# Feed-forward products in another order, and 32-byte pads in four pools

## The chip, the cores and the metric

One Trainium2 chip, one core of it. The metric is the time of one execution on the device in microseconds (us). A core has five engines with queues of their own: PE (TensorE, matrix products; PEld is its loading of weights, which overlaps), DVE (VectorE), ACT (ScalarE), POOL (GpSimd) and SP (SyncE, which here issues most transfers). Each engine takes its instructions strictly in its own order, and waits where an operand isn't there.

## The reference

Two blocks over 512 positions of width 1024, in float32. The first block projects the normed input (`p = h @ w_in`), runs a causal convolution of width 31 with a layer norm, an RWKV scan over 16 heads, and three output products. The second block has two layers, each of attention and of a feed-forward part:

```python
def conv_ffn(h, w_up, conv_w, conv_b, w_down):
    Tp = h.shape[1]
    u = h @ w_up
    up = jnp.pad(u, ((0, 0), (CONV_W - 1, 0), (0, 0)))
    c = conv_b + sum(up[:, j:j + Tp] * conv_w[j] for j in range(CONV_W))
    gate, val = jnp.split(c, 2, axis=-1)
    return (jax.nn.silu(gate) * val) @ w_down
```

`w_up` is 1024 x 5632 and `w_down` 2816 x 1024; the convolution has width 3 and runs along the positions.

## The kernel before, in words

Activations lie transposed: 128 channels on the partitions, positions along the row (512 in the first block, 528 with the 16 meta tokens in the second; the last layer computes 512 of them). Each float32 operand is split in two fp32r parts, hi and lo, and a product is three matmuls: lo weights with hi data, hi weights with lo data, hi with hi (`mm3`, L247; the line of the call that issues a matmul is L75). Weights come in tiles of at most 128 x 1024 (`weights`, L204): SP loads `wst`, ACT casts it to `wh` (L212), POOL subtracts to get `wl` (L215). There are 2, 3 and 3 buffers of these, so a tile's cast waits until the tile three before it has been used up.

The first block (`block1`) multiplies with 512 columns at a time. Its moving operands are the tiles `hx` (the normed input, for the 73 output tiles of `w_in`, the first seven of which are named `pg` in the trace), `ch`, `yo` and `mx` (the operands of `w_conv_out`, `w_rwkv_out` and `w_out`). While these run, the convolution is made on DVE (`cy<-u,vec,cy`, 30 instructions for each of 8 tiles) and the RWKV scan on all engines, in small steps that wait for each other.

`ffn` (L1565) runs once per layer. Its 44 tiles of `w_up` are taken in pairs j = 0 to 21: a gate tile into the PSUM banks `g` and a value tile into the banks `pt`, two banks each. DVE scales them out of PSUM into `u` (L163), ACT and DVE make the convolution `c` (L176, then L173 twice), ACT the tanh `t`, DVE and POOL the product (`t<-t,c` on POOL, L163), ACT casts it to the hi part of `f` (L1604) and DVE subtracts to get the lo part (L163). `f` has 26 buffers, 13 pairs. The inner dimension is done in two parts of 11 pairs: 11 times up, then 8 output tiles m of `w_down`, then again 11 times up and 8 output tiles. One output tile is 11 steps of the inner dimension, in two weight tiles of 6 and 5 steps (128x768 and 128x640), with three matmuls per step: 66 matmuls of 264 columns in layer 0, 33 of 512 columns in layer 1. The tiles m alternate between the banks `g` and `pt`; `add_h` adds a finished one to the residual on DVE. The order of PE in the second block is that of the program; the other engines' order comes from a scheduler.

SBUF is shared out by pools that lie one behind the other, and a tile takes a multiple of 32 bytes per partition. In the built program `hx`, `ch`, `yo` and `mx` of the first block start 32 bytes past a multiple of 64, and all tiles `f` at a multiple of 64.

Of the kernel before, what the change touches and what calls it, by code (L numbers as in the profile page):

```python
# [7 lines left out]
F32 = mybir.dt.float32  # L8
F32R = mybir.dt.float32r
AF = mybir.ActivationFunctionType  # L10
OP = mybir.AluOpType
# [3 lines left out]
P = 128  # L15
S = 512
NT = 8
# [10 lines left out]
NF = 2 * D_FF // P  # L28
# [104 lines left out]
class Kern:  # L133
    def __init__(self, ctx, tc, A, dump):
        self.ctx, self.tc, self.nc, self.A, self.dump = ctx, tc, tc.nc, A, dump
        self.pe = Weave(tc.nc)
        nc = self.nc
        self.cp = ctx.enter_context(tc.tile_pool(name="cp", bufs=1))
        self.vec = self.cp.tile([P, NVEC], F32, name="vec")
        self.con = self.cp.tile([P, NCON], F32, name="con")  # L140
        self.mhalf = self.cp.tile([P, 1], F32, name="mhalf")
        nc.vector.memset(self.mhalf, -0.5)

    def load(self):
        self.nc.sync.dma_start(self.con, self.A["con"])
# [191 lines left out]
def block1(K):  # L337
    nc, tc, A = K.nc, K.tc, K.A
# [31 lines left out]
    hx = []  # L370
    with tc.tile_pool(name="ps0", bufs=1, space=PSUM) as ps0:
# [3 lines left out]
        with tc.high_priority(offset=150000):  # L375
# [3 lines left out]
            for q in range(2):  # L379
                p = pg[5 + q]  # L380
                nc.tensor.matmul(p, one[0:1], row[:, q * 512:(q + 1) * 512], start=True, stop=True)
                th = K.slot("e")
# [19 lines left out]
        for k in range(NT):  # L402
            with tc.high_priority(offset=120000 if k < 2 else 0):
# [3 lines left out]
                gs, sh, x = gsc[:, k:k + 1], mod[:, k:k + 1], xs[k]  # L407
                stt(gs, mod[:, 8 + k:9 + k], 1.0, K.v("norm_g", k), OP.add, OP.mult)
                if k < 2:
                    stt(x, x, gs, rstd, OP.mult, OP.mult)  # L410
                    hi, lo = K.slot("hx", F32R), K.slot("hx", F32R)
# [9 lines left out]
                wh, wl = K.weights(A["w_in0"][k], lo="p")  # L421
# [75 lines left out]

    K.pe.finish(norm)
    ch = [conv.out_gate(i, cog[i]) for i in range(NT)]
    m_ = []  # L500
    for i in range(NT):
        th = K.slot("sq")
# [12 lines left out]
    for i in range(NT):  # L515
        th = K.slot("th")
# [140 lines left out]
class Rwkv:  # L657
# [41 lines left out]
    def close(self):  # L699
        self.rctx.close()  # L700
# [245 lines left out]
    def done(self, what, i):  # L946
        s = self.streams.get((what, i))
        return i < 0 or s is not None and s.done
# [83 lines left out]
class Block2:  # L1032
# [193 lines left out]
    def tl(self, tag, bufs, shape=(P, T), dt=F32):  # L1226
        return self.ap.tile(list(shape), dt, name=tag, tag=tag, bufs=bufs)
# [337 lines left out]
    def ffn(self, l, hx, acc, done):  # L1565

        K, nc, A = self.K, self.nc, self.A
        o = N_META if l else 0
        n, o2 = T - o, max(o - 2, 0)
        mid = (o + T) // 2  # L1570
        hin = [slice(o2, mid), slice(mid, T)]
        hout = [slice(0, n)] if n <= 512 else [slice(0, n // 2), slice(n // 2, n)]
        rb = K.slot("rb")
        p0 = self.first(self.rstd(acc, rb), (A["w_up"][l, 0], hx), (A["w_up"][l, 1], hx), halves=hin)
        with self.tc.tile_pool(name=f"ff{l}", bufs=1, reuse_waits="tile") as fp:
            def tl(tag, bufs, w=n, dt=F32):
                return fp.tile([P, w], dt, name=tag, tag=tag, bufs=bufs)

            half = NF // 4
            banks = self.g, self.pt  # L1580
            for part in range(2):
                fx = []
                for j in range(part * half, (part + 1) * half):
                    c = []
                    for q in range(2):
                        p = p0[q] if j == 0 else self.gemm(A["w_up"][l, 2 * j + q], hx, bank=banks[q], halves=hin)
                        u = tl("u", 3, n + 2)
                        if o == 0:
                            nc.gpsimd.memset(u[:, 0:2], 0.0)
                        for ph, sl in zip(p, hin):  # L1590
                            K.tt(u[:, sl.start + 2 - o:sl.stop + 2 - o], ph, rb[:, sl], OP.mult)
                        f = j + q * (NF // 2)
                        cw = [K.v("conv_w_2", (l * 3 + t) * NF + f) for t in range(3)]
                        x = tl("c", 4)
                        K.act(x, u[:, 2:], AF.Identity, bias=K.v("conv_b_2", l * NF + f), scale=cw[2])
                        K.stt(x, u[:, 0:n], cw[0], x, OP.mult, OP.add)
                        K.stt(x, u[:, 1:n + 1], cw[1], x, OP.mult, OP.add)
                        c.append(x)
                    th = tl("t", 2)
                    K.act(th, c[0], AF.Tanh, scale=0.5)  # L1600
                    K.stt(th, th, 1.0, c[0], OP.add, OP.mult)
                    K.tt(th, th, c[1], OP.mult, "p")
                    hi, lo = tl("f", 26, dt=F32R), tl("f", 26, dt=F32R)
                    nc.scalar.copy(hi, th)  # L1604
                    K.tt(lo, th, hi, OP.subtract)
                    fx.append((hi, lo))
                k0, kn = part * half, 6
                for m in range(NT):
                    ps = [banks[m % 2]()[:, :n // len(hout)] for _ in hout]
                    for a, b in ((0, kn), (kn, half)):  # L1610
                        wh, wl = K.weights(A["w_down"][l, m][:, (k0 + a) * P:(k0 + b) * P], lo="p")
                        for q in zip(ps, hout):
                            K.gemm([q], wh, wl, fx[a:b], first=a == 0, last=b == half)
                    self.add_h(m, ps, 0.5, o)
                    if part == 1:
                        done(m)


    def layer_b(self, hq, acc):
# [249 lines left out]
def body(tc, A, out, dump=None, stop=None):  # L1869
    with ExitStack() as ctx:  # L1870
        K = Kern(ctx, tc, A, dump)
        K.wb = (2, 3, 3)
        K.wp = ctx.enter_context(tc.tile_pool(name="wp", bufs=3))
        K.rw = ctx.enter_context(tc.tile_pool(name="rw", bufs=1))
        K.rd = ctx.enter_context(tc.tile_pool(name="rd", bufs=1, space=DRAM))
        if stop == 2:
            hp = K.hp = ctx.enter_context(tc.tile_pool(name="hp", bufs=1, side="right"))
            K.h = [hp.tile([P, T], F32, name=f"h{i}") for i in range(NT)]
            K.hxt = (ctx.enter_context(tc.tile_pool(name="hxp", bufs=1, side="right", reuse_waits="tile")), T, 16)
            K.load()  # L1880
            K.b1 = ExitStack()
            p0 = K.b1.enter_context(tc.tile_pool(name="b0", bufs=1))
            with tc.tile_pool(name="b1", bufs=1, space=PSUM) as p1:
                bank = lambda: p1.tile([P, 512], F32, name="p", tag="p", bufs=2)
                bias_rows(K, p0.tile([P, 1024], F32, name="st"), bank)
                meta(K, bank)
            K.tags = {"acc": (p0, S, 2), "sq": (p0, S, 2)}
            st = dict(acc=("acc", "acc"), sq="sq", x=[])
            for i in range(NT):
                tc.nc.sync.dma_start(K.h[i][:, N_META:], A["x1"][i])  # L1890
                start(K, st, i)
        else:
            st = block1(K)
        if stop == 1:
            K.b1.close()
            return
        block2(K, out, ctx, st)
# [111 lines left out]
```

## Time and profile before

| | us |
|---|---|
| median of 3 runs | 2368.82 (2368.64 to 2380.41) |
| the profiled execution | 2374.06 |
| its span, first to last instruction | 2372.1 |
| PE busy | 2166.3 (91%) |
| DVE, POOL, ACT busy | 1503.0, 1180.5, 875.4 |

The span is one execution's trace, on which everything below rests; about 2 us lie around it. "Busy" of PE is a sum over pipelined matmuls, so it hides short gaps. The first block takes about the first 916 us, layer 0's feed-forward part runs from about 1186 to 1590 us and layer 1's from about 1970 to the end.

### The profile page before, as it was taken

What the parts mean: (1) busy time and instruction counts of PE and PEld (TensorE: products, weight loads), DVE (VectorE), ACT (ScalarE), POOL (GpSimd) and SP (SyncE); (2) the same over time, 40 slices, a digit from 0 to 9 for tenths busy, and PEclk for the clock granted to TensorE, in tenths of its full rate; (3) what the DMA queues carried; (4) which work ended last, traced back from release to release, by engine and by line L of the source; (5) the groups of instructions that cost most, each with busy time, mean ns of one, the idle gap of its engine ahead of it and who ended that gap; (6) DMA issues with size and microseconds to landing.
All of it is one profiled execution on the core that took longest, in us unless ns stands there. A gap on an engine that the chain in (4) does not pass through costs nothing. (4 is left out here: it accounts for less than half of the span.)

```text
span 2372.1 us, 38579 instructions
## 1 busy us (share of the span) xinstructions
PE 2166.3 (91%) x15069; PEld 1883.9 (79%) x15069; DVE 1503.0 (63%) x2675; ACT 875.4 (37%) x1739; POOL 1180.5 (50%) x989
## 2 busy tenths in 40 slices
PE   5998989997999998998999899898668899989989
PEld 4766766764677777997999899897568799979987
DVE  8477986899972476998466346531366766642661
ACT  3333232332243333535333223332255663332331
POOL 5485556566634446344545445463433345444443
PEclk9998999998999999999999999999789999999999
DMA  7522222222343654220222232232211012223223
GB/s 252 163 71 61 63 83 61 64 68 56 87 154 126 240 167 135 73 63 10 65 82 84 79 97 85 71 102 73 60 58 43 31 63 90 82 78 108 81 76 102
DMA packets 114540, 213.86 MB, mean 90 GB/s; under 512 B 47229, under 2 KB 50813, under 8 KB 114358
## 3 DMA queue, kind: packets, MB, share of 16 engines
q1 hardware_dynamic: 111380, 208.29, 28.1%
q10 hardware_dynamic: 2978, 3.10, 0.4%
q8 instruction: 119, 1.95, 0.3%
q14 instruction: 63, 0.52, 0.1%
HBM read 193.32 MB, written 20.64 MB: 90 GB/s over the span
## 5 line engine op out<-in xcount | busy, mean ns | idle before, releaser
L215 POOL TENSOR_TENSOR wl<-wst,wh 128x1024 fp32r<-128x1024 f32 (+4 forms) x315 | 704.7, 2238 | 725.6 <-ACT wh L212 595.7
L75 PE MATMUL g<-hx,wh 128*128 128x264 f32 (+3 forms) x3680 | 883.3, 329 | 6.6 <-DVE hx L173 6.6
L75 PEld LDWEIGHTS g<-hx,wh 128*128 128x128 f32 x3680 | 622.8, 195 | 62.8 <-issue 11.7
L75 PE MATMUL g<-hx,wl 128*128 128x264 f32 (+3 forms) x1840 | 600.0, 329 | 35.1 <-DVE u L173 9.5
L212 ACT CAST wh<-wst 128x1024 fp32r<-128x1024 f32 (+4 forms) x315 | 304.4, 966 | 421.3 <-PE g L75 223.7
L75 PEld LDWEIGHTS g<-hx,wl 128*128 128x128 f32 x1840 | 356.3, 195 | 61.4 <-issue 11.1
L173 DVE SCALAR_TENSOR_TENSOR c<-u,vec,c 128x528 f32<-128x528 f32 (+1 forms) x176 | 244.7, 1391 | 83.3 <-ACT c L176 81.6
L75 PE MATMUL pt<-hx,wh 128*128 128x264 f32 (+2 forms) x1504 | 271.6, 283 | 0.0
L173 DVE SCALAR_TENSOR_TENSOR cy<-u,vec,cy 128x512 f32<-128x512 f32 x240 | 239.0, 1004 | 3.8
L75 PEld LDWEIGHTS pt<-hx,wh 128*128 128x128 f32 x1504 | 230.2, 189 | 0.0
L75 PE MATMUL pt<-hx,wl 128*128 128x264 f32 (+2 forms) x752 | 207.5, 285 | 10.9 <-DVE u L163 10.8
L75 PEld LDWEIGHTS pt<-hx,wl 128*128 128x128 f32 x752 | 139.2, 189 | 13.2 <-POOL wl L215 10.0
L75 PE MATMUL g<-f,wh 128*128 128x264 f32 (+1 forms) x528 | 123.5, 329 | 2.9 <-DVE f L163 2.9
L75 PE MATMUL pt<-f,wh 128*128 128x264 f32 (+1 forms) x528 | 121.3, 324 | 0.0
L75 PE MATMUL g<-f,wl 128*128 128x264 f32 (+1 forms) x264 | 87.0, 330 | 20.3 <-ACT f L1604 20.3
L75 PEld LDWEIGHTS g<-f,wh 128*128 128x128 f32 x528 | 90.5, 195 | 11.1 <-DVE f L163 4.5
L75 PEld LDWEIGHTS pt<-f,wh 128*128 128x128 f32 x528 | 89.6, 192 | 7.4
L1604 ACT CAST f<-t 128x528 fp32r<-128x528 f32 (+1 forms) x44 | 27.6, 627 | 181.1 <-POOL t L163 96.2
L163 POOL TENSOR_TENSOR t<-t,c 128x528 f32<-128x528 f32 (+1 forms) x44 | 57.5, 1307 | 67.0 <-DVE c L173 67.0
L75 PE MATMUL pt<-f,wl 128*128 128x264 f32 (+1 forms) x264 | 85.8, 325 | 0.0
L176 ACT ACTIVATE t<-c 128x528 f32<-128x528 f32 (+1 forms) x44 | 28.1, 638 | 139.9 <-DVE c L173 139.9
L163 DVE TENSOR_TENSOR f<-t,f 128x528 fp32r<-128x528 f32 (+1 forms) x44 | 35.3, 802 | 68.7 <-ACT f L1604 68.7
(411 smaller groups left out, 3849.8 us busy)
## 6 DMA issues: line engine op xcount, KB each, us to landing
wst<-in_w_up SPq DMA_DIRECT2D x88, 512.0 KB
wst<-in_w_in SPq DMA_DIRECT2D x66, 512.0 KB
ast<-in_ada_w SPq DMA_DIRECT2D x24, 512.0 KB
wst<-in_w_down SPq DMA_DIRECT2D x32, 384.0 KB
wst<-in_w_down SPq DMA_DIRECT2D x32, 320.0 KB
wst<-in_w_in_a SPq DMA_DIRECT2D x17, 512.0 KB
wst<-in_w_kv_b SPq DMA_DIRECT2D x16, 512.0 KB
hrb<-rw_d SPq DMA_DIRECT2D x18, 264.0 KB
```

The lines of the kernel that those rows point to most:

```text
L75: self.nc.tensor.matmul(out, lhsT, rhs, **kw)
L163: (self.nc.vector if eng == "v" else self.nc.gpsimd).tensor_tensor(out, a, b, op)
L173: self.nc.vector.scalar_tensor_tensor(out, a, s, b, op0=o1, op1=o2, accum_out=accum)
L176: self.nc.scalar.activation(out, a, f, bias=bias, scale=scale, accum_out=accum)
L212: nc.scalar.copy(wh[:, :n], st[:, :n])
L215: (nc.vector if lo == "v" else nc.gpsimd).tensor_tensor(wl[:, :n], st[:, :n], wh[:, :n], OP.subtract)
L1604: nc.scalar.copy(hi, th)
```

## The change

`up(j)`, `open_down`, `weights`, `down` and `close` are the old loop's parts as functions. Then:

1. Twelve pairs go up ahead of the first part's output tiles, not eleven; the twelfth (j = 11) belongs to the second part. After these tiles come the ten pairs that are left.
2. In the second part the output tiles m = 0 and 1 both take steps 0 to 9 of the inner dimension, and then the last step each; their four weight tiles are asked for in one go.
3. `line` takes 32 bytes of a pool, and POOL sets them to zero: in `rw` (after which everything in the left half of SBUF lies 32 bytes further), in `cv` (where `ch` lies) and in `ff0` and `ff1` (the pools of `ffn`, where `f` lies). Four such instructions are added.

In the built program the moving operands `hx`, `ch`, `yo` and `mx` of the first block now start at a multiple of 64 bytes, all 2328 matmuls that read them; `f` starts there as before, and the operands of 264, 258 and 256 columns stand where they stood with respect to 64. No other instruction changes its place on its engine, apart from single swaps of neighbours.

```diff
--- before.py
+++ after.py
@@ -140,6 +140,10 @@
         self.con = self.cp.tile([P, NCON], F32, name="con")
         self.mhalf = self.cp.tile([P, 1], F32, name="mhalf")
         nc.vector.memset(self.mhalf, -0.5)
+
+    def line(self, pool):
+
+        self.nc.gpsimd.memset(pool.tile([P, 8], F32, name="line"), 0.0)
 
     def load(self):
         self.nc.sync.dma_start(self.con, self.A["con"])
@@ -497,6 +501,7 @@
 
     K.pe.finish(norm)
     ch = [conv.out_gate(i, cog[i]) for i in range(NT)]
+    K.line(cv)
     m_ = []
     for i in range(NT):
         th = K.slot("sq")
@@ -1576,44 +1581,80 @@
             def tl(tag, bufs, w=n, dt=F32):
                 return fp.tile([P, w], dt, name=tag, tag=tag, bufs=bufs)
 
+            K.line(fp)
             half = NF // 4
             banks = self.g, self.pt
+
+            def up(j):
+
+                c = []
+                for q in range(2):
+                    p = p0[q] if j == 0 else self.gemm(A["w_up"][l, 2 * j + q], hx, bank=banks[q], halves=hin)
+                    u = tl("u", 3, n + 2)
+                    if o == 0:
+                        nc.gpsimd.memset(u[:, 0:2], 0.0)
+                    for ph, sl in zip(p, hin):
+                        K.tt(u[:, sl.start + 2 - o:sl.stop + 2 - o], ph, rb[:, sl], OP.mult)
+                    f = j + q * (NF // 2)
+                    cw = [K.v("conv_w_2", (l * 3 + t) * NF + f) for t in range(3)]
+                    x = tl("c", 4)
+                    K.act(x, u[:, 2:], AF.Identity, bias=K.v("conv_b_2", l * NF + f), scale=cw[2])
+                    K.stt(x, u[:, 0:n], cw[0], x, OP.mult, OP.add)
+                    K.stt(x, u[:, 1:n + 1], cw[1], x, OP.mult, OP.add)
+                    c.append(x)
+                th = tl("t", 2)
+                K.act(th, c[0], AF.Tanh, scale=0.5)
+                K.stt(th, th, 1.0, c[0], OP.add, OP.mult)
+                K.tt(th, th, c[1], OP.mult, "p")
+                hi, lo = tl("f", 26, dt=F32R), tl("f", 26, dt=F32R)
+                nc.scalar.copy(hi, th)
+                K.tt(lo, th, hi, OP.subtract)
+                return hi, lo
+
+            def open_down(m):
+                return [banks[m % 2]()[:, :n // len(hout)] for _ in hout]
+
+            def weights(part, m, a, b):
+                k0 = part * half
+                return K.weights(A["w_down"][l, m][:, (k0 + a) * P:(k0 + b) * P], lo="p")
+
+            def down(ps, w, fx, a, b, c, first=False, last=False):
+
+                for q in zip(ps, hout):
+                    K.gemm([q], *w, fx[a:b], first=first, last=last, k0=a - c)
+
+            def close(part, m, ps):
+                self.add_h(m, ps, 0.5, o)
+                if part == 1:
+                    done(m)
+
+            kn = 6
+            fx = [up(j) for j in range(half + 1)]
             for part in range(2):
-                fx = []
-                for j in range(part * half, (part + 1) * half):
-                    c = []
-                    for q in range(2):
-                        p = p0[q] if j == 0 else self.gemm(A["w_up"][l, 2 * j + q], hx, bank=banks[q], halves=hin)
-                        u = tl("u", 3, n + 2)
-                        if o == 0:
-                            nc.gpsimd.memset(u[:, 0:2], 0.0)
-                        for ph, sl in zip(p, hin):
-                            K.tt(u[:, sl.start + 2 - o:sl.stop + 2 - o], ph, rb[:, sl], OP.mult)
-                        f = j + q * (NF // 2)
-                        cw = [K.v("conv_w_2", (l * 3 + t) * NF + f) for t in range(3)]
-                        x = tl("c", 4)
-                        K.act(x, u[:, 2:], AF.Identity, bias=K.v("conv_b_2", l * NF + f), scale=cw[2])
-                        K.stt(x, u[:, 0:n], cw[0], x, OP.mult, OP.add)
-                        K.stt(x, u[:, 1:n + 1], cw[1], x, OP.mult, OP.add)
-                        c.append(x)
-                    th = tl("t", 2)
-                    K.act(th, c[0], AF.Tanh, scale=0.5)
-                    K.stt(th, th, 1.0, c[0], OP.add, OP.mult)
-                    K.tt(th, th, c[1], OP.mult, "p")
-                    hi, lo = tl("f", 26, dt=F32R), tl("f", 26, dt=F32R)
-                    nc.scalar.copy(hi, th)
-                    K.tt(lo, th, hi, OP.subtract)
-                    fx.append((hi, lo))
-                k0, kn = part * half, 6
-                for m in range(NT):
-                    ps = [banks[m % 2]()[:, :n // len(hout)] for _ in hout]
-                    for a, b in ((0, kn), (kn, half)):
-                        wh, wl = K.weights(A["w_down"][l, m][:, (k0 + a) * P:(k0 + b) * P], lo="p")
-                        for q in zip(ps, hout):
-                            K.gemm([q], wh, wl, fx[a:b], first=a == 0, last=b == half)
-                    self.add_h(m, ps, 0.5, o)
-                    if part == 1:
-                        done(m)
+                f, m0 = fx[:half], 0
+                if part == 0:
+
+                    fx = fx[half:]
+                else:
+
+                    two = []
+                    for m in range(2):
+                        ps, w = open_down(m), weights(1, m, 0, kn)
+                        down(ps, w, f, 0, kn, 0, first=True)
+                        w = weights(1, m, kn, half)
+                        down(ps, w, f, kn, half - 1, kn)
+                        two.append((ps, w))
+                    for m, (ps, w) in enumerate(two):
+                        down(ps, w, f, half - 1, half, kn, last=True)
+                        close(1, m, ps)
+                    m0 = 2
+                for m in range(m0, NT):
+                    ps = open_down(m)
+                    down(ps, weights(part, m, 0, kn), f, 0, kn, 0, first=True)
+                    down(ps, weights(part, m, kn, half), f, kn, half, kn, last=True)
+                    close(part, m, ps)
+                if part == 0:
+                    fx += [up(j) for j in range(half + 1, 2 * half)]
 
 
     def layer_b(self, hq, acc):
@@ -1872,6 +1913,7 @@
         K.wb = (2, 3, 3)
         K.wp = ctx.enter_context(tc.tile_pool(name="wp", bufs=3))
         K.rw = ctx.enter_context(tc.tile_pool(name="rw", bufs=1))
+        K.line(K.rw)
         K.rd = ctx.enter_context(tc.tile_pool(name="rd", bufs=1, space=DRAM))
         if stop == 2:
             hp = K.hp = ctx.enter_context(tc.tile_pool(name="hp", bufs=1, side="right"))
```

Where layer 1's first part ends, on PE. The names: `hx` is the normed input, `f_19836` and `f_19837` are hi and lo of pair 0. Before:

```order
L75 MATMUL pt_21140<-hx_19677,wl_21111 128x256
L75 MATMUL pt_21140<-hx_19678,wh_21110 128x256
L75 MATMUL pt_21140<-hx_19677,wh_21110 128x256
L75 MATMUL g_21180<-f_19836,wl_21183 128x512
L75 MATMUL g_21180<-f_19837,wh_21182 128x512
L75 MATMUL g_21180<-f_19836,wh_21182 128x512
```

And now, behind the same product (pair 10's second tile):

```order
L75 MATMUL pt_21148<-hx_19683,wl_21119 128x256
L75 MATMUL pt_21148<-hx_19684,wh_21118 128x256
L75 MATMUL pt_21148<-hx_19683,wh_21118 128x256
L75 MATMUL g_21194<-hx_19396,wl_21190 128x258
L75 MATMUL g_21194<-hx_19397,wh_21189 128x258
L75 MATMUL g_21194<-hx_19396,wh_21189 128x258
```

The 96 matmuls of pair 11 have moved in between pair 10 and the first output tile.

Where the first output tile of layer 1's second part ends, on PE. `f_23026` is the hi part of pair 21 before, `f_23034` now; `g_` and `pt_` are the output tiles m = 0 and 1. Before:

```order
L75 MATMUL g_23030<-f_22892,wh_23056 128x512
L75 MATMUL g_23030<-f_23026,wl_23057 128x512
L75 MATMUL g_23030<-f_23027,wh_23056 128x512
L75 MATMUL g_23030<-f_23026,wh_23056 128x512
L75 MATMUL pt_23078<-f_21686,wl_23081 128x512
```

And now the end of tile 1's steps 0 to 9 and what follows:

```order
L75 MATMUL pt_23081<-f_22900,wh_23107 128x512
L75 MATMUL g_23038<-f_23034,wl_23065 128x512
L75 MATMUL g_23038<-f_23035,wh_23064 128x512
L75 MATMUL g_23038<-f_23034,wh_23064 128x512
L75 MATMUL pt_23081<-f_23034,wl_23108 128x512
L75 MATMUL pt_23081<-f_23035,wh_23107 128x512
L75 MATMUL pt_23081<-f_23034,wh_23107 128x512
L75 MATMUL g_23134<-f_21318,wl_23137 128x512
```

The first matmul that reads pair 21 stood 30 matmuls behind the last up product, and stands 60 behind it now.

The same place on POOL, from the last weight tile of `w_up` on. Before (`t_22888` and `t_23022` belong to pairs 20 and 21):

```order
L215 TENSOR_TENSOR wl_22961<-wst_22959,wh_22960 128x1024
L215 TENSOR_TENSOR wl_23033<-wst_23031,wh_23032 128x768
L163 TENSOR_TENSOR t_22888<-t_22888,c_22884 128x512
L215 TENSOR_TENSOR wl_23057<-wst_23055,wh_23056 128x640
L215 TENSOR_TENSOR wl_23081<-wst_23079,wh_23080 128x768
L163 TENSOR_TENSOR t_23022<-t_23022,c_23018 128x512
L215 TENSOR_TENSOR wl_23105<-wst_23103,wh_23104 128x640
```

And now:

```order
L219 TENSOR_TENSOR wl_22969<-wst_22967,wh_22968 128x1024
L219 TENSOR_TENSOR wl_23041<-wst_23039,wh_23040 128x768
L167 TENSOR_TENSOR t_22896<-t_22896,c_22892 128x512
L219 TENSOR_TENSOR wl_23065<-wst_23063,wh_23064 128x640
L219 TENSOR_TENSOR wl_23084<-wst_23082,wh_23083 128x768
L167 TENSOR_TENSOR t_23030<-t_23030,c_23026 128x512
L219 TENSOR_TENSOR wl_23108<-wst_23106,wh_23107 128x640
```

POOL's order there is what it was: tile 0's two weight tiles, tile 1's first, pair 21's product, tile 1's second.

## Rows read from the trace of the kernel before

**Rows 1.** The page: PE's busy time, and its granted clock in 40 slices.

```profile
PE 2166.3 (91%) x15069; PEld 1883.9 (79%) x15069; DVE 1503.0 (63%) x2675; ACT 875.4 (37%) x1739; POOL 1180.5 (50%) x989
...
PEclk9998999998999999999999999999789999999999
```

**Rows 2.** The chain that ended last, from 2307 us: start, length (us), what.

```profile
2307.29 1.81 POOL wl L215
...
2310.53 1.26 POOL t L163
...
2311.81 0.63 ACT f L1604
...
2312.46 1.37 DVE f L163
...
2313.88 1.22 PE g L75 x2
```

**Rows 3.** Waits of PE from 1186 us to the end: total us, times, longest.

```profile
PE g L75 <- ACT f L1604: 20.3, 4, 5.3
PE pt L75 <- DVE u L163: 10.8, 12, 1.1
```

**Rows 4.** Stretches, matmuls that read f: length, PE busy (matmuls), clock, DMA share, GB/s.

```profile
1313.73:1338.34 24.61, 18.48 (x132) 0.86 0.21 59
1338.34:1386.34 48.00, 48.00 (x398) 1.00 0.34 101
1516.38:1541.93 25.55, 19.52 (x132) 0.80 0.19 57
2100.74:2124.29 23.55, 18.04 (x67) 0.86 0.23 70
2300.50:2323.26 22.76, 17.25 (x67) 0.85 0.29 87
2323.26:2368.14 44.88, 44.88 (x199) 1.00 0.34 107
```

**Rows 5.** POOL in order of time behind both layers' second up phase: start, us, [idle before].

```profile
1522.35 1.81 POOL L215 TENSOR_TENSOR wl<-wst,wh 128x768 fp32r<-128x768 f32 x1 [3.19 <-issue]
1525.61 1.29 POOL L163 TENSOR_TENSOR t<-t,c 128x528 f32<-128x528 f32 x1 [1.45 <-DVE c L173]
1526.86 1.54 POOL L215 TENSOR_TENSOR wl<-wst,wh 128x640 fp32r<-128x640 f32 x1
...
2311.74 1.54 POOL L215 TENSOR_TENSOR wl<-wst,wh 128x640 fp32r<-128x640 f32 x1
2316.14 1.84 POOL L215 TENSOR_TENSOR wl<-wst,wh 128x768 fp32r<-128x768 f32 x1 [2.87 <-ACT wh L212]
```

**Rows 6.** ACT in order of time, at layer 1's second part: start, us.

```profile
2315.18 0.83 ACT L212 CAST wh<-wst 128x768 fp32r<-128x768 f32 x1 [2.75 <-PE g L75]
```

**Rows 7.** A stretch of the first block, matmuls that read ch; columns as in rows 4.

```profile
780.00:815.00 35.00, 34.81 (x150) 1.00 0.86 306
```

**Rows 8.** Stretches of the first block: busy PE, PEld, DVE, ACT, POOL.

```profile
59.00:640.00 581.00, 530.11 (x3568) 386.67 (x3569) 474.38 (x720) 180.26 (x364) 351.62 (x418) 0.96 0.27 77
640.00:817.00 177.00, 177.00 (x1053) 134.25 (x1048) 86.66 (x140) 64.83 (x127) 77.78 (x44) 0.99 0.51 171
817.00:916.00 99.00, 93.40 (x384) 74.04 (x383) 76.33 (x91) 38.33 (x57) 55.44 (x31) 0.97 0.48 153
```

**Rows 9.** The same stretches, PE's matmuls with hi weights (wh) alone.

```profile
59.00:640.00 581.00, 300.09 (x860) 0.96 0.27 77
640.00:817.00 177.00, 124.50 (x373) 0.99 0.51 171
817.00:916.00 99.00, 82.69 (x256) 0.97 0.48 153
```

**Rows 10.** The convolution on DVE: its group, and one instruction in order of time.

```profile
L173 DVE SCALAR_TENSOR_TENSOR cy<-u,vec,cy 128x512 f32<-128x512 f32 x240 | 239.0, 1004 | 3.8
...
583.33 0.74 DVE L173 SCALAR_TENSOR_TENSOR cy<-u,vec,cy 128x512 f32<-128x512 f32 x1
```

## The prediction

> **What bounds the kernel now.** I read the page first, then the chain that ended last, PE's waits, and two sorts of stretches. PE is busy 91% of the span and granted nearly full clock in almost every slice, so time is won where PE stands still or where its matmuls take longer than they must [rows 1]. From 1186 us on, PE's largest single wait is for ACT's cast of `f`: 20.3 us in 4 times [rows 3]. These are the four places where the up products end and the output tiles begin (two layers, two parts). The chain shows why: PE is through with pair 21's up products at 2300.5 us, but POOL's product, ACT's cast and DVE's subtraction of that pair end at 2313.8, and only then does PE go on [rows 2].
>
> What such a place costs is read from its first two output tiles. The last six of a part run without a stop: 48.00 us for six in layer 0, 8.00 each, and 44.88 in layer 1, 7.48 each [rows 4]. The first two take 24.61 and 25.55 us in layer 0 and 23.55 and 22.76 in layer 1, where 16.00 and 14.96 would do. That is 8.61 + 9.55 + 8.59 + 7.80 = **34.55 us**, the waiting and the time after it: the granted clock there is 0.80 to 0.86 as a mean, 1.00 in the undisturbed stretches, so after each pause a part of the matmuls ran at 1.2 GHz, not 2.4 [rows 4].
>
> The first block is different: no single wait, but PE busy for 530 of 581 us, then for 177 of 177, then 93 of 99 [rows 8]. There the time of one matmul of 512 columns counts.
>
> **The up pair ahead of the first part's tiles.** Nothing is computed that wasn't. Behind pair 10 come 96 matmuls, some 11.6 us, before PE asks for `f` of pair 10, and another 6 to 7 us of tile 0 before the step that reads it. Pair 10 is complete 13.3 us after its last product in layer 1 (2300.5 to 2313.83) [rows 2, 4], so it is there in time. What is late next is tile 1's weights. In the trace POOL makes tile 1's first `wl` from 2307.29 to 2309.10, 8.60 us behind the last up product [rows 2]; in layer 0 at 1524.16, 7.78 us behind it [rows 5]. The built order has the same order on POOL around the last pair of either part, so I keep these delays. PE gets there after tile 0, at 7.48 us in layer 1: a wait of 1.1. In layer 0 it gets there at 8.00: none. Tile 1's second `wl` ends 12.78 us behind (2313.28) and 12.02 in layer 0 (1528.40) [rows 5], while PE arrives at 8.60 + 18 x 0.2267 = 12.68, or 8.00 + 4.36 = 12.36: 0.1 and none. PE also waits 1.1 us in each of the last pairs of a part, 12 times in all, for DVE to empty `pt` [rows 3]. The first part gets one such pair more, the second one fewer: nothing in sum. The pair kept in `f` makes 12 of 13 pairs live; pair 13 must wait for a slot until the eighth output tile has read pair 0, which PE's order puts ahead of its products anyway.
>
> **The two tiles together in the second part.** Here no up product is left to put in between. Pair 21 is first read 60 matmuls behind the last up product in layer 1 (120 in layer 0), at 13.6 us at the earliest (120 x 0.1212 = 14.5), against 13.3 in layer 1; in layer 0 it is ready sooner, since POOL's `t` ends 10.5 us behind the last up product there (1526.90) and 11.3 in layer 1 (2311.79) [rows 2, 5]. But tile 1's first weights are now wanted earlier, after 30 x 0.2267 = 6.80 us in layer 1 and 60 x 0.1212 = 7.27 in layer 0, and come at 8.60 and 7.78: waits of 1.8 and 0.5. The second `wl` then comes 0.1 us late or not at all, as above. Tile 0's second weight tile stays in use longer, till PE has done its last step. In the built program tile 2's first weights take the buffer of tile 1's first instead, free at 12.7 us; cast and subtraction took 2.80 us from start to end (2315.18 to 2317.98) [rows 5, 6], so they are there at 15.5, and PE wants them at 12.78 + 18 x 0.2267 = 16.9. That hides it, with 1.4 us to spare; without that cover it would cost up to 2.8 us per layer. SP's queue has the three next weight tiles ahead of layer 1's first output transfer, so these transfers wait for nothing new.
>
> Left of the 34.55 us are 1.1 + 0.1 + 1.8 + 0.1 + 0.5 = 3.6 us. I leave nothing for the clock, since pauses of 1.1 us in the up phases stand in slices whose granted clock is 0.9 or more [rows 1]. The reordering gives **31 us**; its bounds are 20 (the two second parts keep 7 us each) and 34.5.
>
> **The pads.** Four writes of 32 bytes on POOL without waits: under 0.5 us, beside other work. The point is where 512 columns start. Matmuls of 512 columns that read `f`, at a multiple of 64 bytes, come every 44.88 / 198 = 226.7 ns [rows 4]. Those that read `ch`, 32 bytes past one, come every 35.00 / 150 = 233.3 ns at the same full clock [rows 7]. The gap, 6.6 ns, is what one more piece of 64 bytes in 32 would make (226.7 x 33 / 32 = 233.8). Since no tile of the trace is read at both offsets, the gap might belong to the place and not the address; I take it for the address. Matmuls that move to a multiple of 64: per hi-weight count half as many lo ones come on top [rows 9], so 1290 from 59 to 640 us, 559 to 817, 384 to 916; the 96 before 59 us wait for loads and count nothing. At 6.6 ns these are 8.5, 3.7 and 2.5 us.
>
> What of that reaches the end? From 640 to 817 us PE never pauses: all 3.7. From 817 to 916 it is busy 94%: 2.4. From 59 to 640 it pauses for 51 us, while DVE is busy 474 of 581 [rows 8]; a faster matmul ahead of a pause only makes the pause longer, unless the awaited chain began with a product. I take half, 4.3. **Sum 10.4 us.** Bounds: 14.7 if all arrives, and 4 us lost if nothing arrives and DVE and POOL happen to meet less well.
>
> The Trainium skill, "SBUF — State Buffer", section "Specifications (TRN2)", gives SBUF lines of 16 bytes. By such lines 2048 bytes fill 128 of them from either offset, and the pads would change nothing. The 6.6 ns between the two rows speak against it, as far as they come from the address; this is rival 1.
>
> **Sum.** 31 + 10.4 = 41.4 us. The profiled execution took 2374.06 us, 5.2 above the median; 2374.06 - 41.4 = 2332.7, and off the median 2368.82 - 41.4 = **2327 us**.
>
> **Rivals.**
> 1. The pads are worth nothing, because the 6.6 ns belong to the first block or because its chains on DVE and ACT set the pace. For it: DVE's 82% up to 640 us. Against it: 177 of 177 us of PE after that. 2368.8 - 31 = 2338 us.
> 2. Tile 1's weights take the place of `f`: if POOL does `t` of the last pair before tile 1's first `wl`, this comes not 8.6 but about 12.8 us behind the last up product, 4.2 later at each of four places, and the clock falls there as before. 31 + 10.4 - 17 = 25 us won, 2344 us. Against it: the built order of POOL.
> 3. All of it arrives: 34.5 + 14.7 = 49 us, 2320 us.
> 4. The change doesn't cover what it should: DVE runs behind PE at the end of every up phase [rows 3], so with a twelfth pair it gets further behind, and PE waits for banks what it waited for `f`. Then the two first parts win nothing, and with pads of little use some 10 us are left: 2359 us, not to be told from no change.
> 5. Slower than before: the shifted first block meets worse on DVE and POOL. A convolution instruction took 0.74 us where it ran undisturbed and 1004 ns on average, so 240 of them hold 63 us of standing still [rows 10]. These would have to become 104 us, all of it on the path, before the 41 us are used up; at twice as much the time is 2368.8 - 41 + 63 = 2391. Nothing in the rows says that 32 bytes do this.
>
> **How the numbers follow.** Forecast 0.58 (own range 2321 to 2335), rival 1 0.14, rival 2 0.10, rival 3 0.10, rival 4 0.06, rival 5 0.02. The range from 2318 to 2346 us takes in the forecast, rivals 1 to 3 and the bounds of both terms. About 0.5% (11.8 us) is what a measurement of this kernel tells from no change: faster by more 0.92, within it 0.06, slower by more 0.02.
>
> **What would show it.** Right: PE's waits for the cast of `f` are gone from the list, the first two output tiles of each part take 16 to 18 us, the granted clock there is near 1.00; matmuls of 512 columns that read `ch` come every 226 to 228 ns; the stretch from 640 to 817 us is some 4 us shorter. Wrong: `ch` at 233 ns (rival 1, first form); 227 ns, but PE's pauses before 640 us longer by the same amount (its second form); waits of 4 us and more for `wl` behind the up products (rival 2); more than 1.2 us per late pair for DVE's `u` (rival 4); a convolution instruction well over 1004 ns on average (rival 5).

## The result, and the profile after

The changed kernel takes 2336.55 us (median of 4 runs, 2332.57 to 2338.61), the kernel before 2368.73 in the same comparison. The ratio is 0.985, with a 95% interval of 0.982 to 0.988: 32 us won, where 41.4 were forecast. A second comparison (6 and 11 runs, below) gave 2338.74 against 2372.24, a ratio of 0.9856 (0.9834 to 0.9879). The profiled execution took 2336.27 us, its span is 2334.4, 37.7 less than before.

The page, PE's line and its granted clock, to be held against [rows 1]:

```profile
PE 2143.4 (92%) x15069; PEld 1872.5 (80%) x15069; DVE 1500.7 (64%) x2675; ACT 875.6 (38%) x1739; POOL 1183.1 (51%) x993
...
PEclk9999999998999999999999999998789999999999
```

The waits of PE from 1186 us on, against [rows 3] (total, times, longest):

```profile
PE pt L75 <- DVE u L167: 10.4, 12, 1.1
PE pt L75 <- POOL wl L219: 2.7, 3, 1.5
```

The 20.3 us for ACT's cast of `f` are gone from the list. The twelve waits for `u` are what they were, and a wait for tile 1's weights is new, 1.5 us at the longest.

Stretches of the matmuls that read `f`, against [rows 4]: the first two output tiles and the last six, of layer 0's first part, layer 0's second (the first two only), and layer 1's two parts. The columns are length, PE busy (matmuls), clock, DMA share, GB/s:

```profile
1314.47:1330.58 16.11, 16.11 (x132) 1.00 0.27 72
1330.58:1378.90 48.32, 48.32 (x398) 1.00 0.37 106
1496.48:1513.25 16.77, 16.36 (x133) 1.00 0.25 68
2087.53:2104.02 16.49, 15.74 (x66) 1.00 0.28 82
2104.02:2149.34 45.32, 45.32 (x199) 1.00 0.38 114
2267.97:2285.10 17.13, 15.59 (x66) 1.00 0.27 79
2285.10:2330.19 45.09, 45.09 (x198) 1.00 0.38 120
```

The first two tiles now take 16.11, 16.77, 16.49 and 17.13 us, before 24.61, 25.55, 23.55 and 22.76: 30.0 us less in sum, with the clock at 1.00 where it was 0.80 to 0.86. But layer 1's last six take 45.32, not 44.88: its `f` products have become slower, by 1%, though the prediction left them untouched. Layer 0's first part shows the same on a smaller scale, 48.32 where it was 48.00.

The wait that is left, at the start of layer 1's second part: ACT, POOL and PE in order of time (start, us, and the idle time before with what ended it):

```profile
2273.24 0.63 ACT L180 ACTIVATE t<-c 128x512 f32<-128x512 f32 x1 [2.42 <-DVE c L177]
2273.78 0.82 ACT L216 CAST wh<-wst 128x768 fp32r<-128x768 f32 x1
...
2274.74 1.81 POOL L219 TENSOR_TENSOR wl<-wst,wh 128x768 fp32r<-128x768 f32 x1 [2.92 <-issue]
...
2276.60 0.50 PE L75 MATMUL pt<-f,wl 128*128 128x512 f32 x1 [1.54 <-POOL wl L219]
```

ACT's cast of tile 1's weights stands behind the tanh of pair 21 and waits with it for DVE's `c`. POOL's product for `t` is not in the way. Tile 2's first `wl` starts at 2282.05 and takes 1.85; PE wants it at 2285.10, so the cover held with 1.2 us to spare.

In the first block, `ch` over 35 us, against [rows 7], and the convolution's group, against [rows 10]:

```profile
769.00:804.00 35.00, 34.81 (x154) 1.00 0.84 302
```

```profile
L177 DVE SCALAR_TENSOR_TENSOR cy<-u,vec,cy 128x512 f32<-128x512 f32 x240 | 230.7, 970 | 3.8
```

154 matmuls where there were 150: 227.3 ns each by this count. A convolution instruction takes 970 ns, not more than the 1004 of before.

Every experiment left a trace too. This table gives the length of six stretches, each from the start of one matmul to the start of another, the same two matmuls in every kernel (the last one runs to the end of the span). The stretches bear the times that they have in the trace of before:

| us | 59-640 | 640-817 | 817-950 | 1288-1590 (layer 0, feed-forward) | 1590-1978 (layer 1, attention) | 2075-2372 (layer 1, feed-forward) |
|---|---|---|---|---|---|---|
| before | 580.9 | 176.9 | 133.1 | 302.0 | 388.1 | 297.2 |
| before_again | 581.7 | 178.1 | 132.6 | 301.8 | 388.4 | 298.5 |
| pads_alone | 577.7 | 174.5 | 133.3 | 301.8 | 388.2 | 299.3 |
| order_alone | 577.9 | 176.9 | 135.9 | 284.6 | 392.8 | 284.3 |
| order_again | 581.1 | 176.9 | 133.7 | 284.6 | 388.1 | 284.4 |
| first_part_only | 577.7 | 174.5 | 131.7 | 292.8 | 387.2 | 290.9 |
| two_tiles_only | 571.6 | 174.5 | 133.4 | 293.4 | 386.4 | 292.5 |
| the changed kernel | 573.6 | 174.5 | 133.1 | 284.9 | 391.3 | 285.4 |
| changed_again | 574.0 | 174.8 | 131.8 | 285.0 | 391.3 | 285.2 |
| f_192 | 573.5 | 174.8 | 133.1 | 284.9 | 385.2 | 284.4 |
| f_64 | 573.5 | 176.1 | 132.1 | 284.9 | 391.1 | 286.7 |
| f_128 | 574.1 | 175.9 | 133.6 | 284.9 | 389.4 | 287.1 |
| weights_32 | 578.5 | 176.7 | 136.6 | 285.3 | 391.4 | 287.0 |
| both_32 | 577.2 | 176.0 | 130.4 | 285.3 | 388.1 | 285.2 |

The feed-forward stretches repeat to 1 or 2 us, those of the first block and the attention scatter by 3 to 8 from one execution to the next.

### The profile page after: what moved, and what is told of

Same layout as the page of the kernel before. It is cut to its first block, busy times and chain, and to the rows that moved or that the text cites. A ratio compares the mean times of both kernels' runs of the same rounds, so it can differ in the third digit from the quotient of the medians.

```text
span 2334.4 us, 38589 instructions
## 1 busy us (share of the span) xinstructions
PE 2143.4 (92%) x15069; PEld 1872.5 (80%) x15069; DVE 1500.7 (64%) x2675; ACT 875.6 (38%) x1739; POOL 1183.1 (51%) x993
## 5 line engine op out<-in xcount | busy, mean ns | idle before, releaser
L216 ACT CAST wh<-wst 128x1024 fp32r<-128x1024 f32 (+4 forms) x315 | 304.4, 966 | 391.3 <-PE g L75 187.7
L177 DVE SCALAR_TENSOR_TENSOR cy<-u,vec,cy 128x512 f32<-128x512 f32 x240 | 230.7, 970 | 3.8
L75 PE MATMUL pt<-hx,wl 128*128 128x264 f32 (+2 forms) x752 | 207.9, 285 | 10.6 <-DVE u L167 10.4
L75 PEld LDWEIGHTS pt<-hx,wl 128*128 128x128 f32 x752 | 139.5, 189 | 12.9 <-POOL wl L219 9.0
```

What stands on the lines that cost most here:

```text
L75: self.nc.tensor.matmul(out, lhsT, rhs, **kw)
L177: self.nc.vector.scalar_tensor_tensor(out, a, s, b, op0=o1, op1=o2, accum_out=accum)
L216: nc.scalar.copy(wh[:, :n], st[:, :n])
```

## The experiments

### The two halves of the change, each by itself

`pads_alone`, the kernel before with the four pads:

```diff
+    def line(self, pool):
+        self.nc.gpsimd.memset(pool.tile([P, 8], F32, name="line"), 0.0)
...
+    K.line(cv)
...
+            K.line(fp)
...
+        K.line(K.rw)
```

> The four pads, with the output tiles in the old order. Theory A (the two halves of the change add up, and what the traces of before and after show in the first block is the pads' doing): 10 to 12 us less than before, all of it before 1190 us, so 2357 to 2359 us; ch, yo and mx every 226.8 ns, hx 229 to 230 ns, both feed-forward parts as long as before, their four waits for f back at about 5 us each. Layer 1's f products also stand at another address now (a multiple of 256 bytes instead of 192 past one): if the address made them 229 to 230 ns in the changed kernel, they are that here too (1 to 1.5 us in all); if the new order made them so, they are 226.8 here. Layer 1's attention took 3.2 us longer in the changed kernel: if the shifted addresses did that, it is 3 us longer here too, and the time is 2361. Rival B (the first block's gain has nothing to do with the pads, but is the scatter of its waits): ch at 227 ns, and yet 2364 us or more.

`order_alone`, the changed kernel without them:

```diff
-    K.line(cv)
...
-            K.line(fp)
...
-        K.line(K.rw)
```

> The new order of the feed-forward products without the four pads. Theory A (the halves add up): 29 to 31 us less than before, 2338 to 2340 us, layer 0's part 17 us shorter and layer 1's 12 to 13 us; the first block as before, to 1 or 2 us, with ch at 233 ns; f at 226.8 ns in layer 1 if its address decides, 229 to 230 if the order does. Layer 1's attention as long as before if the pads made it longer; 3 us longer if it is the order of layer 0's products that did, or chance. Rival C (the pads help the feed-forward part too, or hinder it): a gain there other than 29 by more than 3 us.

The pads alone: 2369.43 us (10 runs) against 2370.35 (13 runs) of before, ratio 0.9989 (0.9975 to 1.0002). By the ratio that is 2.6 us, between 6 won and none (the two medians lie 0.9 apart), where 10 to 12 were expected: a miss, as to size. `ch` came every 227 ns, as expected, and yet the time is above 2364 us, as rival B had it. The order alone: 2345.54 us, ratio 0.9892 (0.9864 to 0.9920), 26 us won where 29 to 31 were expected; its feed-forward stretches are 17.3 us (layer 0) and some 13 to 14 us shorter, which is what was expected, and it lost 4.7 us in layer 1's attention. `f` in layer 1 came every 226.7 ns with the order alone and every 228.9 ns with the pads alone, so its address makes it slower, not the order.

### The two parts of the new order

`first_part_only`, the changed kernel without the two tiles together:

```diff
-                else:
-                    two = []
...
-                    m0 = 2
```

> The changed kernel with the pads and the twelfth up pair ahead of the first part's output tiles, but tiles 0 and 1 of the second part one after the other as before. Theory A (each boundary pays for itself): the two first parts keep what they won, the two second parts lose it: 9.6 us in layer 0 and 5.4 in layer 1, so 2336.5 + 15 = 2351.5 us, with two waits for f of about 5 us behind the last up products. Rival D (one pair fewer in the second up phase lets DVE catch up, so that f is ready sooner there): the waits are 3 us or less, and the time 2346 or less.

`two_tiles_only`, without the twelfth pair ahead:

```diff
-            fx = [up(j) for j in range(half + 1)]
+            fx = [up(j) for j in range(half)]
...
-                    fx += [up(j) for j in range(half + 1, 2 * half)]
+                    fx += [up(j) for j in range(half, 2 * half)]
```

> The changed kernel with the pads and the two output tiles summed together in the second part, but eleven up pairs ahead of the first part's tiles as before. Theory A: the first parts lose the 7.3 and 5.3 us that they won in the changed kernel's trace, the second parts keep theirs, so 2336.5 + 12.6 = 2349 us; waits for f of 4 to 5 us at the two first parts only. Rival E (in the second parts the pair only shifts the wait to the weights of tile 1, and most of the gain there comes from the twelfth pair): gains in the second parts of under 10 us in sum, and 2354 or more.

2351.04 us (0.9918, 0.9891 to 0.9945) and 2348.55 us (0.9911, 0.9879 to 0.9944), against 2351.5 and 2349 expected. Waits of PE from 1186 us on, first with the twelfth pair alone, then with the two tiles alone:

```profile
PE pt L75 <- DVE u L167: 10.5, 12, 1.1
PE g L75 <- ACT f L1610: 10.1, 2, 5.3
```

```profile
PE g L75 <- ACT f L1610: 10.1, 2, 5.2
...
PE pt L75 <- POOL wl L219: 1.9, 2, 1.5
```

Each measure takes away two of the four waits for `f` and leaves the other two at full length, so rivals D and E fall. The gains add up to within 0.6 us: in layer 0 the twelfth pair wins 9.1 us and the two tiles 8.5, both together 17.0; in layer 1 7.4 and 5.8, together 12.9 (table, against the mean of the three kernels in the old order, 301.9 and 298.3).

### The changed kernel and the order alone once more

Unchanged copies, to see what is chance.

> The changed kernel itself once more, to tell what of its trace is chance. Theory A (the new order is worth 28 to 30 us, the pads 2 to 4): 2337 to 2341 us, the feed-forward stretches as in the first trace to 0.5 us; 640 to 817 us of before again 2.4 us shorter; the 5 us won between 206 and 231 us as in every other kernel, since they were a stop of before's profiled execution and not the pads' gain; and layer 1's attention, 3.2 us longer in the first trace, as long as before. Rival (the pads are worth the 9 us by which the changed kernel beat the order alone): the stretch from 59 to 640 us is again 5 us shorter than in the order alone.

> The new order without the pads once more. Theory A: 2 to 4 us above the changed kernel of the same rounds, so 2340 to 2344 us; the 4 us lost in its first trace between 590 and 680 us and 1645 and 1670 us don't all return. Rival (pads worth 9): 2346 us, 9 above the changed kernel.

2338.74 us (6 runs) and 2343.83 us (6 runs, ratio 0.9882, 0.9854 to 0.9910): 5.1 us apart, between the two expectations. Three things missed. Layer 1's attention was 391.3 us again, 3 above before. The stretch from 59 to 640 us was again some 4 to 7 us shorter than in the order alone, as the rival had it. And the 5 us between 206 and 231 us are no peculiarity of one execution of before: `order_again` lost them too.

### What the address does

The pads move the operands by 32 bytes, but also against the weight tiles, which stay at 192 bytes past a multiple of 256. `f_192` was meant to put layer 1's `f` back to where it stood in this respect:

```diff
-    def line(self, pool):
...
+    def line(self, pool, n=8):
...
-            K.line(fp)
+            K.line(fp, 56 if l else 8)
```

(`n` is the number of 4-byte elements.)

> The changed kernel with 224 bytes instead of 32 in the pool of layer 1's feed-forward part, so that its tiles f start at 192 past a multiple of 256 bytes, as before the change, not at a multiple of 256. Theory (the address sets how often a matmul of 512 columns can start): f every 226.7 ns instead of 228.9 to 230 in layer 1, so 528 x 2.4 ns = 1.3 us less, 2335 us by the first runs of the changed kernel, and nothing else moves. Rival (the order of the products, or the memory next to it, does it): 229 again and the same time.

`weights_32` leaves the operands where the change put them, and moves the weights:

```diff
         K.wp = ctx.enter_context(tc.tile_pool(name="wp", bufs=3))
+        nc = tc.nc
+        nc.gpsimd.memset(K.wp.tile([P, 8], F32, name="line", tag="line", bufs=1), 0.0)
         K.rw = ctx.enter_context(tc.tile_pool(name="rw", bufs=1))
-        K.line(K.rw)
```

> The changed kernel with the pad of rw put into the pool of the weight tiles instead, ahead of them: the moving operands stay where the change put them, the weight tiles wst, wh and wl move to 32 bytes past a multiple of 64. Theory M (the moving operand's address alone counts): ch, yo and mx at 226.8 ns, f at 229, time as the changed kernel. Theory D (the distance of the moving operand from the weights, modulo 64, counts): ch, yo and mx at 233 ns as before the change, f above 233, about 8 us more.

`both_32` moves both:

```diff
-        s = tl("so", 6, (P, 1))
+        s = tl("so", 5, (P, 1))
...
         K.wp = ctx.enter_context(tc.tile_pool(name="wp", bufs=3))
+        nc = tc.nc
+        nc.gpsimd.memset(K.wp.tile([P, 8], F32, name="line", tag="line", bufs=1), 0.0)
```

> The changed kernel with one 32-byte pad more, in the pool of the weight tiles, so that the weights and the moving operands hx, ch, yo and mx all start 32 bytes past a multiple of 64 (to make room, a 4-byte tile of layer 1's attention has 5 buffers instead of 6). Theory D (their distance counts, and it is a multiple of 256 here): ch, yo and mx at 226.8 ns, hx at 229 to 230, f (64 bytes off the weights, modulo 256, as in the changed kernel) at 229, 2336 to 2341 us. Theory O (an operand of either kind that lies off a multiple of 64 costs): 233 ns or more everywhere, 2345 us or more.

The same 97 distances between `ch` matmuls (from the 48th to the 145th of 192), at the full clock, in the changed kernel, `weights_32` and `both_32` (columns as above):

```profile
773.43:795.44 22.01, 22.01 (x98) 1.00 0.84 299
```

```profile
780.97:803.60 22.63, 22.63 (x98) 1.00 0.85 293
```

```profile
777.84:800.47 22.63, 22.63 (x98) 1.00 0.89 311
```

And of `yo`, in `both_32` and `weights_32`:

```profile
826.71:848.70 21.99, 21.99 (x99) 1.00 0.45 124
```

```profile
832.49:855.13 22.64, 22.64 (x99) 1.00 0.43 122
```

22.0 us are 226.8 ns each, 22.63 are 233.3. In `weights_32` the data lie at multiples of 64 and yet take the slow pace: a start on a multiple of 64 bytes is not what counts. In `both_32`, `yo` and the weights both lie 32 bytes past a multiple of 64, and the pace is the fast one: an odd 32 costs nothing, so theories M and O fall. `ch` is the exception in `both_32`: its pool lies elsewhere and did not move, so it stood 32 bytes from the weights, and the text of the expectation, which counts it among the moved, is wrong there. As the only operand of the first block left at another distance it is the only one that stayed slow. What counts is the distance of the moving operand from the weights. The times go the same way: `weights_32` took 2351.44 us (1 run), 12.7 above the changed kernel where some 8 were expected, and `both_32` 2336.37 (4 runs, ratio 0.9838, 0.9806 to 0.9869), in the range of theory D.

How far that goes, `f` in layer 1 tells, with the same edit as `f_192` and other numbers (24 and 40 elements):

> The changed kernel with 96 bytes instead of 32 in the pool of layer 1's feed-forward part: f starts 64 past a multiple of 256, the weights at 192 as always, a distance of 128. If the distance counts modulo 128: 226.7 ns, as at distance 0. If it counts modulo 256 or more: another value than 226.7, at most 229 to 230.

> The changed kernel with 160 bytes instead of 32 in that pool: f starts 128 past a multiple of 256, 192 from the weights, modulo 256. If the distance counts modulo 128: 228.9 ns, as at distance 64, where the changed kernel's f lies. If it is the multiple of 256 (the absolute address) that is slow: 226.7.

Five output tiles of layer 1's second part, 165 matmuls, in `f_192`, the changed kernel, `both_32`, `f_64`, `f_128` and `weights_32`:

```profile
2278.10:2315.50 37.40, 37.40 (x166) 1.00 0.45 138
```

```profile
2285.10:2322.87 37.77, 37.77 (x166) 1.00 0.44 136
```

```profile
2286.60:2324.37 37.77, 37.77 (x167) 1.00 0.44 136
```

```profile
2286.18:2324.53 38.35, 38.35 (x167) 1.00 0.43 134
```

```profile
2287.38:2325.87 38.49, 38.49 (x166) 1.00 0.43 134
```

```profile
2299.40:2337.90 38.50, 38.50 (x166) 1.00 0.44 134
```

| start of f less start of the weights, modulo 256 | 0 | 64 | 128 | 192 | 32 |
|---|---|---|---|---|---|
| one matmul of 512 columns, ns (stretch / 165) | 226.7 | 228.9 | 232.4 | 233.3 | 233.3 |

So neither of the two expected rules holds. The distance doesn't count modulo 128, since 0 and 128 differ. And a start at a multiple of 256 is not slow as such: in `both_32` `f` starts 32 past one, at the same distance of 64 as in the changed kernel, and takes the same 228.9 ns. In the built programs `f` in layer 1 stands at a distance of 0 modulo 512 before the change and of 256 in `f_192`, and takes 226.7 ns in both, so for this value 256 is the period; for the others it was not tried. Before the change `f` stood at distance 0, and `hx`, `ch`, `yo` and `mx` at 32 or 224. The pads brought these four to 0, and `f` from 0 to 64. `f_192` has all five at 0 (`f` in layer 1). It took 2334.69 us (6 runs), ratio 0.9842 (0.9818 to 0.9867), beside 2338.74 of the changed kernel in the same rounds, and is the fastest kernel here by its median; 2335 had been expected. The intervals overlap, and of the 4 us between the two medians `f` explains 1; what its trace shows for certain is layer 1's feed-forward stretch, 284.4 us against 285.4 and 285.2. `f_64` took 2338.03 us and `f_128` 2339.42 (1 run each).

### The kernel before, once more

> The kernel before once more, to tell what of its trace is chance. Between 206 and 231 us it took 25.0 us, as did one of two runs of the order alone, with a granted clock of 0.50 for 10 us behind a pause of PE of 2.5 us; the kernels with moved operands took 19.6 to 20.6. If the clock falls there by chance: 25.0 or 19.6. If it falls whenever the operands lie 32 bytes off, since PE then comes to that place otherwise: 25.0. From 59 to 640 us 578 to 581 us, from 640 to 817 176.9.

Between 206 and 231 us it took 22.1 us, neither 25.0 nor 19.6; 581.7 and 178.1 us in the two other stretches. The whole execution took 2377.05 us. So the time there changes from one execution of the same program to the next. Where the 25 us come from, PE's rows show, in the kernel before, in `order_again` and in `order_alone`, from 200 to 205 and from 205 to 215 us (PE busy, clock):

```profile
200.00:205.00 5.00, 2.75 (x44) 0.89 0.65 170
205.00:215.00 10.00, 10.00 (x59) 0.50 0.24 72
```

```profile
200.00:205.00 5.00, 2.72 (x31) 0.81 0.67 209
205.00:215.00 10.00, 10.00 (x57) 0.50 0.20 55
```

```profile
200.00:205.00 5.00, 5.00 (x60) 1.00 0.74 210
205.00:215.00 10.00, 10.00 (x83) 1.00 0.22 56
```

Where PE paused for 2.3 us, the next 10 us ran at 1.2 GHz; in the third execution, of the same program as the second, it didn't pause and kept 2.4 GHz. Two of the five traces whose `hx` stands at another distance than 0 have this pause and none of the nine at distance 0, where PE's longest pause in that place is 1.2 us; whether that is chance too is not shown.

## Why the prediction was right, and where it wasn't

The forecast was 2327 us, and the time, 2336.55, lies in its wide range, 2318 to 2346, and on the side that it gave 0.92. It is 1.6 us outside the forecast's own range, 2321 to 2335, which had 0.58.

**The boundaries.** 34.55 us were there, 31 were to be won. The first two tiles of the four places fell by 30.0 us in the trace, from 96.47 to 66.50. The forecast was 3.6 us above 61.9, all of it waits; measured are 4.6, of which 2.7 are waits and 1.9 lie in PE's busy time, 0.3 of them through the slower `f` of layer 1. For tile 1's weights PE waits 1.5 us in layer 1's second part (1.8 expected), 0.4 in layer 0's (0.5 expected) and 0.8 in layer 1's first (1.1 expected). Nothing was left for the clock, and it is 1.00. The reason given for the wait was half right: POOL's order is as read from the program, but the delay comes from ACT, where the cast stands behind a tanh.

**The pads, size.** The terms were 4.3, 3.7 and 2.4 us. Means over the five executions whose `hx` stands at distance 224 and the nine at distance 0 (table): 580.0 to 574.8 from 59 to 640 us, 5.3 won; 177.1 to 174.9 from 640 to 817 (without `both_32`, whose `ch` is slow), 2.1 won; 134.4 to 132.5 from there to 950, 1.9 won. But the prediction counted its third term to 916 us, and behind that no matmul reads these four operands: up to there the means are 99.5 and 99.3, 0.3 won, and the other 1.6 are not the pads' pace. In the predicted stretches the pads thus won 7.7 us, not 10.4. The third term failed as the prediction itself had feared for the first: from 817 to 916 us PE stood still 5.6 us at distance 224 and 7.2 at distance 0 (means of the same traces), so faster matmuls ahead of the pauses before `yo` and `mx` mostly made the pauses longer. In the changed kernel the stretch of the same matmuls is this, against 99.00 and 93.40 in [rows 8]:

```profile
806.30:906.10 99.80, 92.46 (x384) 0.95 0.51 156
```

The second term was mis-sized because 6.6 ns is the price of a long series. `ch` gained it in full (760 to 817: 56.76 to 55.32 us in the two first traces). `hx` stands in short series between the small products of the scan, and there only the eighth and later matmul of a series comes every 227 to 228 ns. The first takes some 337 ns in both traces; the next six take 229 to 232.5 after the change and 232 to 234 before it (starts of neighbouring matmuls). Without the first, the mean went from 232.8 to 229.6 ns, half of what was counted. In the first term this didn't show, and that was luck: 1290 matmuls at 3.2 ns give 4.1 us if all of it arrives, so a part of the 5.3 is something else, such as the 10 us at 1.2 GHz above.

**The pads, mechanism.** Wrong. "One more piece of 64 bytes in 32" reproduced the 6.6 ns by its numbers and is refuted by `weights_32` and `both_32`: the same data at a multiple of 64 were slow, and 32 bytes off it fast. The sum came near all the same, because the same pads brought the distance of four operands to 0. By the wrong rule `f` was safe, as it stayed on a multiple of 64; in fact it went from distance 0 to 64 in layer 1, whose feed-forward part gave 0.9 us back (285.3 against 284.4). The Trainium skill, "SBUF — State Buffer", section "Specifications (TRN2)", gives lines of 16 bytes; by them none of these kernels should differ in pace, since each distance is a multiple of 16, and the rows above, from 226.7 to 233.3 ns, decide against that as the whole account.

**The sum.** By stretches, 30 and 7.7 less 0.9 were won, against 31 and 10.4. The traces of the changed kernel also show layer 1's attention 3 us longer, both times, which no step had foreseen. It was 385.2 to 392.8 in the other kernels with the new order and 386.4 to 388.4 in those without the whole of it, so the new order may have a part in it; that stays open. It lies chiefly in two of PE's waits there, of 8.0 and 7.9 us (8.2 and 8.1 in `changed_again`), which are 5.8 and 7.0 before and 6.0 and 7.1 in `f_192`, with the same order of products. Of the 9.5 us between forecast and time, then, 3.6 are the pads with `f` (6.8 net against 10.4), 1 the boundaries and 3 the attention. The other 2 are what is left over. They fit the step "off the median", which took a gain read from a slow execution off the median of faster ones: the two traces lie 37.8 us apart, the medians 32.2. The profiled executions of before (2374.06 and 2377.05 us) stand above the medians of before (2368.7 to 2373.0), those of the changed kernel (2336.27 and 2336.48) don't. A part of what the traces give as won in the first block is then the slow end of before's scatter, such as the 10 us at 1.2 GHz. How much the pads are worth over many executions stays unsettled: 2.6 us alone, with an interval that takes in none; on top of the new order 5.1 us in the same comparison, with intervals that overlap, and 9.0 by the first runs of both kernels, which were not made together.

**The rivals.** Rival 1, in its first form, fell (`ch` at 227 ns). Its second form, longer pauses, holds from 817 to 916 us and in part before 640, where PE stood still 48.9 us at distance 224 and 51.2 at 0 (means). Its time, 2338, was nearer than the forecast, mostly by other means. Rival 2: the longest wait for `wl` is 1.5 us, not 4. Rival 3: 32 us won, not 49. Rival 4: the waits for `u` are still 1.1 us at the most and twelve in number. Rival 5: 970 ns.

## What to carry to other kernels

Where a stage reads what a chain over four engines has only just made, put products without that dependence in between, or open a second sum: here the waits cost 5.5 to 6.1 us at each of four places (length less PE busy in [rows 4]) and the lower clock after them another 2.3 to 3.5 (PE busy above the undisturbed pace), and both went at once. Before costing an address, change the two operands' places separately: a single pair of rows at different addresses (226.7 and 233.3 ns) gave the price of the effect but not its cause, and the wrong cause slowed the operand that had been right. And when one trace is the base of a sum, say how far its execution lies from the median, and take the loss to be in the stretches that scatter.

## What the hardware showed that was not expected

The pace of fp32r matmuls with 512 columns hangs on the distance between the moving operand and the weights in SBUF, modulo 256 bytes (as a period this is shown for 0 alone): 226.7 ns at 0, 228.9 at 64, 232.4 at 128, 233.3 at 192, at 32 and at 224. Distance 0 was fast at two places (both at 192, both at 224 past a multiple of 256), distance 64 took 228.9 ns at two (`f` at 0 and at 32 past one), and every matmul has its own weights loaded beside it (15069 of either on the page). Why the two meet is not shown. Nor is the start of a series: behind matmuls of other shapes the first that reads `hx` took some 337 ns at distance 0 and at 224, the next six 229 to 232.5 at distance 0, and only those behind them 227 to 228.
